# Inside a decoder layer: the order of an attention step, scores first and the turn of the probabilities last

## The chip, the cores and the metric

One core of a Trainium2 chip runs the whole kernel in one launch. The metric is the device time of one execution in microseconds (us); the kernel before was timed in three runs. Below, PE is the matrix engine and PEld its weight loads, DVE the vector engine, ACT the scalar engine, POOL the GpSimd engine and SP the queue that issues most DMAs.

## The reference

One decoder layer on 256 tokens with 16 learned meta tokens in front (T = 272 rows, width 2048, float32): a SwiGLU block, a merge of two mixers (differential attention and a short gated convolution), a second SwiGLU block, a last norm. The change lies in the attention. It has 8 heads, and each head has two score maps of 64-wide queries and keys and values 128 wide:

```
s = einsum('bqhcd,bkhcd->bchqk', q_blk, kp) * scale      # c = 0, 1
s = where(mask, s, NEG_INF)
p = softmax(s, axis=-1)
a = p[:, 0] - lam * p[:, 1]
out = einsum('bhqk,bkhv->bqhv', a, vp)
```

Before and after it stand plain matrix products: `h @ w_in` makes q, k, v and the three inputs of the convolution.

## The kernel before

**Dense products.** `linear` (L305) multiplies a 2048-deep activation with 512 columns of a weight matrix. Per 128-deep chunk it issues 12 matmuls (L367, L368, L369 for each of 4 column groups), because every float32 operand is split into a rounded high part and a low part. The weights come by DMA into `st`; for each block of two chunks ACT writes the high part `wh` (L351) and DVE the low part `wl` (L356), each in a ring of three buffers. A finished product stays in four of the eight PSUM banks until the next `linear` reaches its second chunk, where it is evicted (`flush`).

**Attention as side work.** The attention doesn't have a stage of its own. `side` is a list of small functions, and `linear` takes one from it after the chunks named in `side_at`, mostly every third chunk, so that a piece of attention lies after every 36 dense matmuls. The list holds 18 attention steps: the work is cut into 16 units, one for each head and each block of 128 queries (`qt` = 0 or 1), and step i works on three units at once (`att_step`, L999). Before the change it first multiplies the probabilities of unit i-2 with the values (`values`, L934), then transposes the probabilities of unit i-1 (`turn`, L919), and then makes the scores of unit i (`scores`, L889). The dense products in which these steps lie are the second k, the second v, and the first and second pair c and u of the convolution's inputs.

**A unit.** `scores` issues two matmuls on PE, one for each score map, with 64 rows of the array each (L896, out `sc_ps`); then DVE scales and masks them (L899, two instructions) and takes the row maxima (L903); ACT takes two exponentials with row sums (L906); DVE takes the reciprocals (L910), multiplies one with lambda (L911), scales the second map (L912) and combines the two maps by two instructions of line L914: one writes the 16 meta columns into `scM`, where four heads and both query blocks are gathered, and the other writes the 128 or 256 remaining columns back into `sc`. `turn` transposes these columns on PE (L923, out `aT`: one transpose for `qt` = 0, two for `qt` = 1) and ACT copies them to `aB` (L927). In the last unit of each group of four heads it also transposes `scM` (L925), which `meta_values` needs later. `values` multiplies `aB` with the values on PE (L938, out `po`: one or two matmuls), and DVE copies the result out (L939).

**What sets the order.** The program isn't run in the order in which it is written. A scheduler takes the instructions of each engine by the order in which they were recorded, but an instruction that by its own estimate isn't ready yet can be passed by later ones. On the chip each engine then works through its list in order and waits at semaphores. Pools with a fixed number of buffers (two for `sc`, eight PSUM banks for all products) add waits of their own.

Of the kernel before, what the change touches and what calls it, by code (L numbers as in the profile page):

```python
# [18 lines left out]
NMETA = 16  # L19
# [41 lines left out]
def decoder_layer(ctx: ExitStack, tc: tile.TileContext, t, out):  # L61
# [9 lines left out]
    def bank(name):  # L71
        return psum.tile([P, 512], F32, tag="acc", name=name)
# [579 lines left out]
    def mixed(plan, a, w, cols, name, end):  # L652

        ev = {}

        def done(k, ps):
            if k == "x":
                ev["u"] = wide([P, 2, GW], "u2x")
                nc.scalar.copy(out=ev["u"][:, 1, :], in_=ps)
            elif k == "3":  # L660
                ev["p3"] = ps
            elif k == "1":
                ev["e"], ev["g"] = wide([P, 2, GW], "cup"), wide([P, 2, GW], "cgate")
                nc.scalar.copy(out=ev["e"][:, 0, :], in_=ps)
            if k in "x31":
                return
            up, gt, u = ev["e"], ev["g"], ev["u"]
            if k == "2":
                nc.vector.tensor_add(gt[:, 0, :], ps, up[:, 0, :])
            elif k == "6":  # L670
                nc.vector.tensor_add(u[:, 0, :], ps, up[:, 0, :])
            elif k == "4":
                nc.vector.tensor_add(gt[:, 1, :], ps, u[:, 0, :])
            elif k == "5":
                nc.vector.tensor_sub(up[:, 0, :], ps, u[:, 0, :])
                nc.vector.tensor_add(up[:, 1, :], up[:, 0, :], u[:, 1, :])
                nc.vector.tensor_add(up[:, 0, :], ev["p3"], up[:, 0, :])
            elif k == "7":
                nc.vector.tensor_add(gt[:, 1, :], ps, gt[:, 1, :])
                nc.vector.tensor_sub(up[:, 1, :], up[:, 1, :], ps)  # L680

                pending.append(lambda: end(gt, up))

        linear_mix(plan, a, w, cols, name, done)
# [131 lines left out]
    def k_evict(g):  # L816
        def f(ps):
            kT[g] = apool.tile([P, GC, T], F32, tag="act", name=f"kT{g}")
            for j in range(GC):
                nc.vector.tensor_mul(kT[g][:, j, :], ps[j][:, :T], norm2.rstd)  # L820

        return f
# [23 lines left out]
    def v_evict(g):  # L846
        def f(ps):
            vt = wide([P, GC, T], "vt")
            for j in range(GC):
                nc.vector.tensor_mul(vt[:, j, :], ps[j][:, :T], norm2.rstd)  # L850
            steps = []

            def meta():
                vz = wide([P, GC, 2, GC, NMETA], "vz")
                nc.vector.memset(vz, 0.0)
                pa = bank("pa")
                for j in range(GC):
                    for i in range(2):
                        nc.vector.tensor_copy(vz[:, j, i, j, :], vt[:, j, :NMETA])
                    nc.tensor.transpose(  # L860
                        pa[:, j * P : (j + 1) * P], vz[:, j, :, :, :].rearrange("p i c m -> p (i c m)"), ident
                    )
                nc.vector.tensor_copy(vB[:, g, :, :].rearrange("p c v -> p (c v)"), pa)

            def real(i):
                pv = bank("pv")
                for j in range(GC):
                    nc.tensor.transpose(pv[:, j * P : (j + 1) * P], vt[:, j, NMETA + i * P : NMETA + (i + 1) * P], ident)
                nc.scalar.copy(out=vN[g][:, i, :, :].rearrange("p c v -> p (c v)"), in_=pv)

            def all_():
                meta()
                real(0)
                real(1)

            side.insert(0, all_)

        return f

    scM = [const.tile([P, 2, GC, NMETA], F32, name=f"scM{g}") for g in range(2)]  # L880
    aM = [None, None]

    class Unit:
# [5 lines left out]
        def scores(self):  # L889
            qt, g, j = self.qt, self.g, self.j  # L890
            nk = NMETA + (qt + 1) * P
            sc = tmp.tile([P, 2, T + NMETA], F32, tag="sc", name="sc")
            for c in range(2):
                rows = slice(c * HD, (c + 1) * HD)
                ps = bank("sc_ps")
                nc.tensor.matmul(  # L896
                    ps[:, :nk], qT[g][rows, j, qt * P : (qt + 1) * P], kT[g][rows, j, :nk], start=True, stop=True
                )
                nc.vector.scalar_tensor_tensor(  # L899
                    out=sc[:, c, :nk], in0=ps[:, :nk], scalar=rq[:, qt : qt + 1], in1=mask[:, T - nk :], op0=ALU.mult, op1=ALU.add  # L900
                )
            mx = tmp.tile([P, 2], F32, tag="mx", name="mx")
            nc.vector.tensor_reduce(out=mx, in_=sc[:, :, :nk], axis=AX.X, op=ALU.max, negate=True)  # L903
            sm = tmp.tile([P, 2], F32, tag="sm", name="sm")
            for c in range(2):
                nc.scalar.activation(  # L906
                    sc[:, c, :nk], sc[:, c, :nk], AF.Exp, bias=mx[:, c : c + 1], accum_out=sm[:, c : c + 1]
                )
            rs = tmp.tile([P, 2], F32, tag="rs", name="rs")
            nc.vector.reciprocal(rs, sm)  # L910
            nc.vector.tensor_mul(rs[:, 1:2], rs[:, 1:2], lam)  # L911
            nc.vector.tensor_scalar_mul(sc[:, 1, :nk], sc[:, 1, :nk], rs[:, 1:2])  # L912
            for out_, ks in ((scM[g][:, qt, j, :], slice(0, NMETA)), (sc[:, 0, NMETA:nk], slice(NMETA, nk))):
                nc.vector.scalar_tensor_tensor(  # L914
                    out=out_, in0=sc[:, 0, ks], scalar=rs[:, 0:1], in1=sc[:, 1, ks], op0=ALU.mult, op1=ALU.subtract
                )
            self.sc = sc
# [23 lines left out]
    def meta_values(g):  # L941
        om = [bank(f"om{qt}") for qt in range(2)]
        for qt in range(2):
            rows = slice(qt * GC * NMETA, (qt + 1) * GC * NMETA)
            nc.tensor.matmul(
                om[qt], aM[g][rows, :], vB[rows, g, :, :].rearrange("p c v -> p (c v)"), start=True, stop=True
            )
        for qt in range(2):
            o = oN[g][:, qt, :, :].rearrange("p c v -> p (c v)")
            nc.vector.tensor_add(o, om[qt], o)  # L950
        head_squares(g, 0)

    def head_squares(g, qt):
        for j in range(GC):
            junk = tmp.tile([P, P], F32, tag="junk", bufs=1, name="junk")
            h = g * GC + j
            nc.scalar.activation(junk, oN[g][:, qt, j, :], AF.Square, accum_out=osq[:, qt, h : h + 1])
# [30 lines left out]
    for g in range(2):  # L988
        dense = dict(side_at=(2, 5, 8, 11, 14) if g else (4, 6, 8, 10, 12))
        linear(h2, allk, w_in, 0, W2 + g * GW, 0, T, "k", k_evict(g), **dense)  # L990
        if g == 0:
            mixed(Q, hm, w_in, (0, GW), "q", q_end)
            mixed(B_PLAN, hm, w_in, (3 * W2, 3 * W2 + GW), "b", b_end)
            dense = dict(later_at=(3, 5, 7, 9))
        linear(h2, allk, w_in, 0, 2 * W2 + g * GW, 0, T, "v", v_evict(g), **dense)
        if g == 0:
            units = [Unit(h, qt) for h in range(NH) for qt in range(2)]

            def att_step(i):  # L999
                def f():  # L1000
                    if 0 <= i - 2 < len(units):
                        units[i - 2].values()
                    if 0 <= i - 1 < len(units):
                        units[i - 1].turn()
                    if i < len(units):
                        units[i].scores()

                return f

            half = len(units) // 2  # L1010
            side.extend(att_step(i) for i in range(half + 2))
            side.append(lambda: meta_values(0))
            side.append(lambda f=att_step(half + 2): [head_squares(0, 1), f()])
            side.extend(att_step(i) for i in range(half + 3, len(units) + 2))
            side.append(lambda: meta_values(1))
            side.append(lambda: [head_squares(1, 1), att_norm()])
            side.extend(att_out(h) for h in range(0, NH, 2))
# [313 lines left out]
```

## Time and profile before

| | |
|---|---|
| median of three runs | 2152.15 us (2152.11 to 2152.21) |
| the profiled execution, its own time | 2152.49 us |
| its span, first to last instruction | 2150.7 us |
| granted PE clock | 0.999 |
| busy: PE, DVE, ACT, POOL | 2139.3, 1612.9, 1104.4, 79.3 us |
| DMA over the span | 439.70 MB, mean 204 GB/s |
| the stretch of the attention steps, 938 to 1075 us: busy PE, DVE, ACT | 135.15, 104.14, 70.34 of 137.00 us |

The profile's rows give a start in us from the span's beginning, a duration, the engine, the line, the operation with its output and inputs, and in brackets the idle time of the engine before it with what ended it. PE's rows start when a matmul starts; its ends are modelled and overlap the next start. A matmul of full float32 operands shows as two rows (x2 for one, x4 for two), a transpose as one, and a dense matmul as one.

### The profile page before, as it was taken

Reading aid. Unit: us, or ns where it says so; the run is one execution under the profiler, and the core shown is the slowest. Engines: PE = TensorE matmul, PEld = TensorE weight load, DVE = VectorE, ACT = ScalarE, POOL = GpSimd, SP = SyncE. Lnnn points to the kernel's source line nnn. Section 1 sums busy time; section 2 is a strip of 40 time slices with the busy share of each in tenths; the row PEclk is TensorE's granted clock in tenths of the full one; section 3 lists DMA queues with packets and bytes.
Section 4 is the critical chain, followed back from the end, with each engine's and each line's share of the span. In section 5 each row is a group of like instructions: output and inputs, shape, how many; then the busy total and the mean of one; then the engine's idle time right before and its main releaser. Section 6 shows DMA issues by size and latency. Waiting matters only on the chain.

```text
span 2150.7 us, 33079 instructions
## 1 busy us (share of the span) xinstructions
PE 2139.3 (99%) x13202; PEld 1929.4 (90%) x13202; DVE 1612.9 (75%) x2139; ACT 1104.4 (51%) x1391; POOL 79.3 (4%) x89
## 2 busy tenths in 40 slices
PE   9999999999999999999999999999999999999998
PEld 9999999999999998898998888888888888888887
DVE  8555554445555668867788888889999899988998
ACT  6344343344443455544545555557665566555665
POOL 0000000000000000000000000001100111002100
PEclk9999999999999999999999999999999999999999
DMA  7555555555555555544455555668886999779963
GB/s 257 176 177 178 177 182 178 179 180 180 181 178 177 177 177 193 179 159 137 157 180 191 196 197 195 215 199 255 271 256 201 287 284 277 233 221 306 291 206 137
DMA packets 200544, 439.70 MB, mean 204 GB/s; under 512 B 10493, under 2 KB 11206, under 8 KB 200390
## 3 DMA queue, kind: packets, MB, share of 16 engines
q1 hardware_dynamic: 184022, 398.13, 54.9%
q0 software_dynamic: 15904, 38.80, 8.2%
q8 instruction: 103, 1.69, 0.3%
q10 hardware_dynamic: 464, 0.66, 0.1%
q14 instruction: 51, 0.42, 0.1%
HBM read 431.26 MB, written 2.10 MB: 201 GB/s over the span
## 4 chain that ended last, share of the span: by engine, by line
PE 96%; DVE 2%; ACT 1%; issue 0%; DMA 0%; SPq 0%; ACTq 0%
PE pg L569 6%; PE pg L571 6%; PE pg L570 6%; PE pd L369 4%; PE pd L367 4%; PE pu L369 4%; PE pu L367 4%; PE pu L368 4%; PE pd L368 4%; PE pg L369 4%; PE pg L367 4%; PE pg L368 4%; PE pd L571 4%; PE pd L569 4%; PE pd L570 4%; PE g L571 2%
## 5 line engine op out<-in xcount | busy, mean ns | idle before, releaser
L356 DVE TENSOR_TENSOR wl<-st,wh 128x1024 fp32r<-128x1024 f32 (+1 forms) x329 | 401.0, 1220 | 374.6 <-ACT wh L351 374.5
L351 ACT CAST wh<-st 128x1024 fp32r<-128x1024 f32 (+1 forms) x328 | 342.9, 1046 | 486.0 <-PE pu L368 151.0
L476 DVE TENSOR_TENSOR wl<-st,wh 128x1024 fp32r<-128x1024 f32 (+1 forms) x424 | 470.6, 1117 | 55.6 <-ACT wh L475 52.5
L475 ACT CAST wh<-st 128x1024 fp32r<-128x1024 f32 (+1 forms) x424 | 400.5, 970 | 209.3 <-PE pdx L570 59.3
L475 ACT CAST wh<-t 128x1024 fp32r<-128x1024 f32 x160 | 166.6, 1052 | 241.9 <-DVE t L609 154.1
L476 DVE TENSOR_TENSOR wl<-t,wh 128x1024 fp32r<-128x1024 f32 x160 | 193.8, 1221 | 56.7 <-ACT wh L475 52.7
L369 PE MATMUL pd<-mh,wl 128*128 128x272 f32 x704 | 203.3, 289 | 0.0
L367 PE MATMUL pd<-mh,wh 128*128 128x272 f32 x704 | 202.5, 288 | 0.0
L367 PE MATMUL pg<-h,wh 128*128 128x272 f32 x704 | 202.0, 288 | 0.4 <-ACT wh L351 0.3
L367 PE MATMUL pu<-h,wh 128*128 128x272 f32 x704 | 202.1, 287 | 0.0
L369 PE MATMUL pu<-h,wl 128*128 128x272 f32 x704 | 201.9, 287 | 0.0
L368 PE MATMUL pu<-h,wh 128*128 128x272 f32 x704 | 201.9, 287 | 0.0
L368 PE MATMUL pg<-h,wh 128*128 128x272 f32 x704 | 201.4, 287 | 0.0
L368 PE MATMUL pd<-ml,wh 128*128 128x272 f32 x704 | 200.9, 285 | 0.0
L369 PE MATMUL pg<-h,wl 128*128 128x272 f32 x704 | 199.9, 288 | 0.1
L570 PE MATMUL pg<-wh,h 128*128 128x512 f32 x399 | 156.1, 391 | 0.0
L569 PE MATMUL pg<-wh,h 128*128 128x512 f32 x399 | 155.9, 391 | 0.0
L571 PE MATMUL pg<-wl,h 128*128 128x512 f32 x399 | 155.8, 391 | 0.0
L367 PEld LDWEIGHTS pg<-h,wh 128*128 128x128 f32 x704 | 132.8, 189 | 1.2 <-ACT wh L351 0.9
L368 PEld LDWEIGHTS pd<-ml,wh 128*128 128x128 f32 x704 | 133.6, 190 | 0.0
L368 PEld LDWEIGHTS pg<-h,wh 128*128 128x128 f32 x704 | 132.7, 188 | 0.2 <-DVE h L232 0.2
L367 PEld LDWEIGHTS pu<-h,wh 128*128 128x128 f32 x704 | 132.7, 188 | 0.0
(391 smaller groups left out, 4841.6 us busy)
## 6 DMA issues: line engine op xcount, KB each, us to landing
st<-in_ffn_w_gu_dram SPq DMA_DIRECT2D x183, 512.0 KB, 6.0
st<-in_ffn_w_down_dram SPq DMA_DIRECT2D x88, 1024.0 KB, 5.1
st<-in_ffn_w_gu_dram SPq DMA_DIRECT2D x84, 1024.0 KB, 4.9
st<-in_w_in_dram SPq DMA_DIRECT2D x48, 1024.0 KB, 5.0
st<-in_w_gate_dram SPq DMA_DIRECT2D x64, 512.0 KB, 4.2
t<-in_ffn_w_gu_dram POOLq DMA_DIRECT2D x64, 512.0 KB, 7.4
st<-in_w_branch_dram SPq DMA_DIRECT2D x32, 512.0 KB, 4.8
st<-in_w_out_dram SPq DMA_DIRECT2D x16, 1024.0 KB, 5.2
```

What stands on the lines that cost most here:

```text
L351: nc.scalar.copy(out=wh[:, :m, :], in_=sw)
L356: nc.vector.tensor_sub(wl[:, :m, :], sw, wh[:, :m, :].bitcast(F32))
L367: nc.tensor.matmul(a, wh[:, i, f], act.part(c, 0, t0, t1), start=first, stop=False)
L368: nc.tensor.matmul(a, wh[:, i, f], act.part(c, 1, t0, t1), start=False, stop=False)
L369: nc.tensor.matmul(a, wl[:, i, f], act.part(c, 0, t0, t1), start=False, stop=last)
L475: part_last[:] = [nc.scalar.copy(out=wh, in_=src).ins]
L476: part_last.append(nc.vector.tensor_sub(wl, src, wh.bitcast(F32)).ins)
L569: nc.tensor.matmul(ps[k], hi, wh, start=first, stop=False)
L570: nc.tensor.matmul(ps[k], lo, wh, start=False, stop=False)
L571: nc.tensor.matmul(ps[k], hi, wl, start=False, stop=left[k] == 0)
```

## The change

In `att_step` the scores of unit i are now recorded first, then the values of unit i-2, and the turn of unit i-1 last. In `scores` the two combinations of L914 change places: the 128 or 256 columns that `turn` reads are written first and the 16 meta columns behind them. Nothing is added or taken away.

```
-            for out_, ks in ((scM[g][:, qt, j, :], slice(0, NMETA)), (sc[:, 0, NMETA:nk], slice(NMETA, nk))):
+            for out_, ks in ((sc[:, 0, NMETA:nk], slice(NMETA, nk)), (scM[g][:, qt, j, :], slice(0, NMETA))):
                 nc.vector.scalar_tensor_tensor(
                     out=out_, in0=sc[:, 0, ks], scalar=rs[:, 0:1], in1=sc[:, 1, ks], op0=ALU.mult, op1=ALU.subtract
                 )
...
             def att_step(i):
                 def f():
+                    if i < len(units):
+                        units[i].scores()
                     if 0 <= i - 2 < len(units):
                         units[i - 2].values()
                     if 0 <= i - 1 < len(units):
                         units[i - 1].turn()
-                    if i < len(units):
-                        units[i].scores()
```

The scheduler carries this through PE's, DVE's and ACT's lists; those of POOL and SP stay as they were. The first place is PE's list at step 6, inside the second v product (`v_...` are its four accumulators, `h_128` the activation chunk). A "+" marks the rows of the changed kernel, a "-" those of before.

```order
 L368 MATMUL v_10133<-h_128,wh 128x272
 L369 MATMUL v_10133<-h_128,wl 128x272
+L896 MATMUL sc_ps<-kT_8874,qT_9204 128x144 x2
 L938 MATMUL po<-vN_8499,aB 128x128
+L923 MATMUL aT<-ident,sc 128x128 x2
 L367 MATMUL v_10130<-h_128,wh 128x272
-L923 MATMUL aT<-ident,sc 128x128 x2
-L896 MATMUL sc_ps<-kT_8874,qT_9204 128x144 x2
 L368 MATMUL v_10130<-h_128,wh 128x272
```

The scores now stand at the head of the step, and one dense matmul that stood ahead of the transposes stands behind them. In eight of the sixteen steps that have a turn the list before had dense matmuls between the step's place and the transposes: 9 in step 1 (ahead of the whole group), then 4, 1, 1, 12, 8, 5 and 3 in steps 2, 6, 8, 12, 13, 14 and 16. In the changed list there are none in any step.

The second place is DVE's list from the end of unit 4's combination to the end of unit 5's, which the transposes of step 6 read. This is the list before:

```order
L356 TENSOR_TENSOR wl<-st,wh 128x1024
L939 COPY oN_8501<-po 128x128
L356 TENSOR_TENSOR wl<-st,wh 128x1024
L899 SCALAR_TENSOR_TENSOR sc<-sc_ps,rq,mask 128x272 x2
L903 TENSOR_REDUCE mx<-sc 128x2
L910 RECIPROCAL rs<-sm 128x2
L911 TENSOR_TENSOR rs<-rs,lam 128x1
L912 TENSOR_SCALAR sc<-sc,rs 128x272
L914 SCALAR_TENSOR_TENSOR scM_8504<-sc,rs 128x16
L914 SCALAR_TENSOR_TENSOR sc<-sc,rs 128x256
```

And this is the same place in the changed kernel:

```order
L356 TENSOR_TENSOR wl<-st,wh 128x1024
L899 SCALAR_TENSOR_TENSOR sc<-sc_ps,rq,mask 128x272 x2
L939 COPY oN_8501<-po 128x128
L903 TENSOR_REDUCE mx<-sc 128x2
L356 TENSOR_TENSOR wl<-st,wh 128x1024
L910 RECIPROCAL rs<-sm 128x2
L911 TENSOR_TENSOR rs<-rs,lam 128x1
L912 TENSOR_SCALAR sc<-sc,rs 128x272
L914 SCALAR_TENSOR_TENSOR sc<-sc,rs 128x256
L914 SCALAR_TENSOR_TENSOR scM_8504<-sc,rs 128x16
```

The copy of `po` and the second split `wl`, which stood ahead of the masking (L899), now stand behind it, the split behind the maxima (L903).

The third place is DVE's list at the end of unit 11's softmax, where the first c product is evicted (L1029, L1030). Before:

```order
L910 RECIPROCAL rs<-sm 128x2
L356 TENSOR_TENSOR wl<-st,wh 128x1024
L911 TENSOR_TENSOR rs<-rs,lam 128x1
L1030 TENSOR_TENSOR cg<-cg,rstd 128x258
L912 TENSOR_SCALAR sc<-sc,rs 128x272
L356 TENSOR_TENSOR wl<-st,wh 128x1024
L914 SCALAR_TENSOR_TENSOR scM_8505<-sc,rs 128x16
L914 SCALAR_TENSOR_TENSOR sc<-sc,rs 128x256
```

And in the changed kernel:

```order
L910 RECIPROCAL rs<-sm 128x2
L1029 TENSOR_TENSOR cg<-c_10512,rstd 128x258
L911 TENSOR_TENSOR rs<-rs,lam 128x1
L1029 TENSOR_TENSOR cg<-c_10513,rstd 128x258
L912 TENSOR_SCALAR sc<-sc,rs 128x272
L1030 TENSOR_TENSOR cg<-cg,rstd 128x258
L914 SCALAR_TENSOR_TENSOR sc<-sc,rs 128x256
L914 SCALAR_TENSOR_TENSOR scM_8505<-sc,rs 128x16
L1030 TENSOR_TENSOR cg<-cg,rstd 128x258
L356 TENSOR_TENSOR wl<-st,wh 128x1024 x2
```

Two splits that stood ahead of the combination now stand behind it.

More of the change, by code (lines that the diff above doesn't have):

```diff
@@ L912, in scores @@
             nc.vector.tensor_scalar_mul(sc[:, 1, :nk], sc[:, 1, :nk], rs[:, 1:2])
-            for out_, ks in ((scM[g][:, qt, j, :], slice(0, NMETA)), (sc[:, 0, NMETA:nk], slice(NMETA, nk))):
+            for out_, ks in ((sc[:, 0, NMETA:nk], slice(NMETA, nk)), (scM[g][:, qt, j, :], slice(0, NMETA))):
                 nc.vector.scalar_tensor_tensor(
@@ L1000, in f @@
                 def f():
+                    if i < len(units):
+                        units[i].scores()
                     if 0 <= i - 2 < len(units):
@@ L1004, in f @@
                         units[i - 1].turn()
-                    if i < len(units):
-                        units[i].scores()
                 return f
```

## Prediction

> **What bounds the kernel now.** I began with the profile's page: the span, the busy time of each engine, and the chain that ended last.
>
> ```profile
> span 2150.7 us, 33079 instructions
> PE 2139.3 (99%) x13202; PEld 1929.4 (90%) x13202; DVE 1612.9 (75%) x2139; ACT 1104.4 (51%) x1391; POOL 79.3 (4%) x89
> PE 96%; DVE 2%; ACT 1%; issue 0%; DMA 0%; SPq 0%; ACTq 0%
> ```
>
> PE is the bound: 96% of the chain is its own. The change adds and removes no matmul, so it can gain only what PE loses between matmuls, and only in the stretch with the attention steps. The second view is the list of what PE waits for.
>
> ```profile
> PE aT L923 <- DVE sc L914: 1.5, 6, 0.5
> ```
>
> In the attention steps it names one wait, that of the transposes of `turn` for the combined probabilities: 1.5 us in 6 steps. The wait is real, but this number is too small, as the third view shows, the timeline of PE's starts. First two steps without a wait, one of each kind: step 3, which makes the scores of a late query block and turns an early one, and step 4, the other way round.
>
> ```profile
> 957.32 0.28 PE L368 MATMUL k<-h,wh 128*128 128x272 f32 x1
> 957.44 0.29 PE L369 MATMUL k<-h,wl 128*128 128x272 f32 x1
> 957.57 0.61 PE L938 MATMUL po<-vN,aB 128*128 128x128 f32 x4
> 958.01 0.27 PE L923 MATMUL aT<-ident,sc 128*128 128x128 f32 x1
> 958.22 0.73 PE L896 MATMUL sc_ps<-kT,qT 64*128 64x272 f32 x4
> 958.88 0.39 PE L367 MATMUL k<-h,wh 128*128 128x272 f32 x1
> 959.10 0.29 PE L368 MATMUL k<-h,wh 128*128 128x272 f32 x1
> ```
>
> ```profile
> 964.91 0.38 PE L938 MATMUL po<-vN,aB 128*128 128x128 f32 x2
> 965.13 0.38 PE L923 MATMUL aT<-ident,sc 128*128 128x128 f32 x2
> 965.44 0.52 PE L896 MATMUL sc_ps<-kT,qT 64*128 64x144 f32 x4
> 965.88 0.39 PE L367 MATMUL v<-h,wh 128*128 128x272 f32 x1
> 966.11 0.28 PE L368 MATMUL v<-h,wh 128*128 128x272 f32 x1
> ```
>
> Read the starts, not the durations, which overlap. A dense matmul starts 0.12 us after the one before it (957.32, 957.44). Step 3 takes 959.10 - 957.57 = 1.53 us with one dense matmul inside, so 1.41 without it: values 0.44, transpose about 0.12, scores 0.85 (0.66, and 0.10 at each border, where 0.21 and 0.22 stand instead of 0.11 and 0.12). Step 4 takes 1.20 - 0.12 = 1.08: values 0.22, transposes 0.21, scores 0.65. Now step 6, which has the work of step 4:
>
> ```profile
> 976.29 0.38 PE L938 MATMUL po<-vN,aB 128*128 128x128 f32 x2
> 976.43 0.37 PE L367 MATMUL v<-h,wh 128*128 128x272 f32 x1
> 977.26 0.41 PE L923 MATMUL aT<-ident,sc 128*128 128x128 f32 x2 [0.46 <-DVE sc L914]
> 977.60 0.52 PE L896 MATMUL sc_ps<-kT,qT 64*128 64x144 f32 x4
> 978.04 0.40 PE L368 MATMUL v<-h,wh 128*128 128x272 f32 x1
> 978.28 0.29 PE L369 MATMUL v<-h,wl 128*128 128x272 f32 x1
> ```
>
> It takes 1.99 us with two dense matmuls, 1.75 without them: 0.67 more than step 4. The row's bracket says 0.46, because it counts from the modelled end of the matmul before. By the same subtraction ten of the sixteen steps with a turn are longer than a step without a wait: steps 2, 6, 7, 8, 11, 12, 13, 14, 15 and 16, by 0.41, 0.67, 0.33, 0.30, 0.47, 0.33, 0.31, 0.36, 0.38 and 0.18 us, 3.7 us in all. The other six have nothing to give. Here are the gaps ahead of the transposes in the first and the last of the ten.
>
> ```profile
> 952.24 0.29 PE L367 MATMUL k<-h,wh 128*128 128x272 f32 x1
> 952.73 0.41 PE L923 MATMUL aT<-ident,sc 128*128 128x128 f32 x2 [0.20 <-DVE sc L914]
> ```
>
> ```profile
> 1049.80 0.28 PE L369 MATMUL u<-h,wl 128*128 128x258 f32 x1
> 1050.06 0.41 PE L923 MATMUL aT<-ident,sc 128*128 128x128 f32 x2
> ```
>
> The last one carries no bracket, though 0.26 lie between the starts and not 0.12. The Trainium skill says the same of the record in "Perfetto Trace Analysis", section "Tensor Engine Instruction (MATMUL, LD_WEIGHTS)": the end time of a TensorE instruction is computed by the profiler, not observed. By idle time as recorded the change could give at most 1.5 us, by the starts 3.7; I take the starts.
>
> **Why the transposes wait.** DVE's timeline from step 5 to step 6 shows the softmax of unit 5.
>
> ```profile
> 971.08 0.29 DVE L939 COPY oN<-po 128x128 f32<-128x128 f32 x1 [0.57 <-PE po L938]
> 971.64 1.23 DVE L356 TENSOR_TENSOR wl<-st,wh 128x1024 fp32r<-128x1024 f32 x1 [0.27 <-ACT wh L351]
> 972.78 0.90 DVE L899 SCALAR_TENSOR_TENSOR sc<-sc_ps,rq,mask 128x272 f32<-128x272 f32 x2
> 973.72 0.72 DVE L903 TENSOR_REDUCE mx<-sc 128x2 f32<-128x544 f32 x1
> 975.69 0.17 DVE L910 RECIPROCAL rs<-sm 128x2 f32<-128x2 f32 x1 [1.25 <-ACT sc L906]
> ...
> 976.48 0.23 DVE L914 SCALAR_TENSOR_TENSOR scM<-sc,rs 128x16 f32<-128x16 f32 x1
> 976.63 0.48 DVE L914 SCALAR_TENSOR_TENSOR sc<-sc,rs 128x256 f32<-128x256 f32 x1
> ```
>
> The combination ends at 977.11 and the transposes start 0.15 us later. In step 2 they would be due at 952.36, in step 6 at 976.63: the chain of scores, maxima, exponentials and combination is some tenths longer than the 36 dense matmuls that lie between two steps, and a split of 1.14 us stands inside it.
>
> **The change, part by part.**
>
> *Meta columns behind the others.* The combination that PE waits for starts 976.63 - 976.48 = 0.15 us sooner in each step. What is late next is the meta columns, later by 0.4; only L925 reads them, in steps 8 and 16, behind two transposes of 0.21. Cost 0 to 0.1 us once or twice; I take nothing.
>
> *Scores first.* In the new step the scores start 0.43 us (965.44 - 964.91 - 0.10) or 0.55 us (958.22 - 957.57 - 0.10) sooner after the step's place, so the softmax can start sooner; and the next transposes stand behind the scores and the values, which cover them with 0.65 or 0.85 us of PE work. Worked through for unit 5, by the new list of DVE, in which the copy and the second split stand behind the masking; PE's row of step 5 and the free case from scores to masking are these. Step 5 begins at 970.43, and PE starts its scores 0.10 later.
>
> ```profile
> 970.43 0.61 PE L938 MATMUL po<-vN,aB 128*128 128x128 f32 x4
> ```
>
> ```profile
> 958.98 0.91 DVE L899 SCALAR_TENSOR_TENSOR sc<-sc_ps,rq,mask 128x272 f32<-128x272 f32 x2 [0.25 <-PE sc_ps L896]
> ```
>
> There the masking starts 0.76 after the scores (958.22), so here at 971.3; the maxima 0.94 later plus 0.25 for the copy, at 972.5; the reciprocal 1.97 after them (975.69 - 973.72; the split of 1.14 fits beside ACT's exponentials), at 974.45; the combination 0.94 - 0.15 later, at 975.25, ready at 975.75 and seen by PE 0.15 later, at 975.9. The transposes come due at 976.29 (the step's place) + 0.65 + 0.22 = 977.15. So they have 1.2 us in hand, where they were late by 0.67. Units with an early block run the same instructions over 144 columns instead of 272, which can only be shorter.
>
> *The dense matmuls that covered the transposes.* Here the new order gives something back: the 4, 1, 1, 12, 8, 5 and 3 dense matmuls that stood ahead of the transposes of steps 2, 6, 8, 12, 13, 14 and 16 now stand behind them. The worst place is step 12 with 12 of them, 1.43 us. There unit 11's chain on DVE also loses two splits (1.14 each) from its middle, as the third place of the order shows, so the combination comes about 2 x 1.14 + 0.15 = 2.4 us sooner and the cover isn't missed. If no chain came sooner at all, each stall would change by the cover lost less the scores that now stand ahead: 0.41 + 0.49 - 0.65 = 0.25 in step 2, then 0.14, 0, 0, 0, 0.33 + 1.43 - 0.65 = 1.11 in step 12, 0.41, 0.31, 0 and 0.54 in step 16, which has no scores: 2.7 us stay of 3.7. That bounds the gain from below at 1.0 us, as far as the waits go.
>
> *New borders on PE.* The scores use 64 rows of the array. Before, they stood between transposes and dense matmuls; now dense matmuls come ahead of them and values behind. The border ahead is in the trace, in step 0:
>
> ```profile
> 941.02 0.29 PE L369 MATMUL k<-h,wl 128*128 128x272 f32 x1
> 941.24 0.52 PE L896 MATMUL sc_ps<-kT,qT 64*128 64x144 f32 x4
> ```
>
> It is 0.22, again 0.10 above a dense start: as before. The border from scores to values isn't in the trace. From below it costs nothing, which would save 0.10 in 15 steps, 1.5 us. From above it adds the weight loads of the two float32 halves of `po`, if neither can be drawn ahead of the scores' end; this is their row in the view by tile (shortest, median and longest in ns):
>
> ```profile
> L938 PEld LDWEIGHTS po<-vN,aB x48: 187/189/193, 951.5 to 1061.7; 128*128 128x128 f32 x48
> ```
>
> That is up to 2 x 0.19 = 0.38 in 14 steps, 5.3 us. I take the usual 0.10, and so no change, since that is what scores into dense cost. The Trainium skill bears on this in "TensorEngine Tiling (Array Packing)", section "Key Properties": changing the tiling mode drains the engine. By that rule each step pays two drains in either order, so the sum stays.
>
> *DVE's and ACT's lists.* The copy of `po` (L939) moves behind the masking, by up to 0.9 us; its reader comes many steps later, and its bank is wanted a step later: nothing. The splits `wl` move back by at most 2.4 us; behind them PE would wait, but each is made with a ring of three blocks of 24 matmuls, and the list of PE's waits names no split: nothing. Were a split late by all of its 2.4 us beyond its ring, that would be lost once. The queues of SP and POOL are untouched.
>
> **The sum.** 3.7 us of stalls, less 0.3 for places with little in hand (step 2, whose whole group also comes 9 dense matmuls sooner after step 0, keeps perhaps 0.1 to 0.3 of its 0.41): 3.4 us. The profiled execution took 2152.49 us (1.8 outside its span), 0.34 above the median of the runs, so 2149.1 for it and 2148.7 us for the median. I call a change under 0.2% (4.3 us) the same, as a measurement of this kernel can tell about that much; the forecast of -0.16% lies within.
>
> **The rivals.**
>
> *The chains come no sooner* (12 in 100). If DVE's splits, which wait for ACT (the bracket at 971.64), held up the masking as they do now, only the cover would count and 1.0 us would be won: 2151.2 us. Against it: in the new list the second split stands behind L899 and L903.
>
> *The scores' border with the values costs more* (5 in 100). A price above 3.4 / 14 = 0.24 us per step turns the gain into a loss. At 0.38, 5.3 - 3.4 = 1.9 us slower, 2154.0. It would show as values starting late after the scores in every step.
>
> *The border is cheaper* (8 in 100). If scores into values cost no border, 1.5 us come on top, and the whole 3.7 us go: 2152.15 - 5.2 = 2146.9, faster by 0.24%.
>
> *The change does nothing* (3 in 100): 2152.1, if PE's gaps at the transposes had another cause than the combination. Against it stands the bracket at 977.26, which names it.
>
> **How the numbers follow.** The forecast with its 3.4 us has 72 in 100. The range reaches from 4.75 us of gain, the forecast with most of the border's 1.5 us, to the rival with 1.0 and a little less: 2147.4 to 2151.4. It leaves out the two borders' full prices and the change that does nothing, 16 in 100, and a few for the tails. Faster by over 0.2% needs 4.3 us, more than all stalls: only the cheap border gives it, 0.08. Slower by over 0.2% needs 7.7 us lost against the forecast, more than the dear border at its full price: 0.02, with a place I have not seen. The rest, 0.90, is the same.
>
> **What would show it.** Right: in the changed profile PE's wait for L914 is gone or under 0.3 us; the even steps take 1.08 and the odd ones 1.41 us of PE beside dense matmuls, with starts 0.44 or 0.66 us apart from scores to values and 0.1 between values and transposes; L899 starts under 0.9 us after the scores. Wrong: gaps of more than 0.2 us ahead of L923 in more than three steps, a gap behind L896 above the usual 0.1, a PE wait for `wl`, or a gain that PE's starts don't account for.

## The result, and the profile after

| | before | changed |
|---|---|---|
| median (all runs), us | 2152.32 (2152.06 to 2152.56) | 2149.17 (2148.85 to 2149.47) |
| ratio | | 0.9985, 95% interval 0.9979 to 0.9992 |
| profiled execution, its span, us | 2152.49, 2150.7 | 2149.04, 2147.3 |

The changed kernel is 3.15 us faster where 3.4 were forecast (2149.17 against 2148.7 us). The kernel before came out 0.17 us higher here than in the three runs from which the forecast starts. The page shows the same kernel as before, with a PE that is a little fuller; these are its span, its first busy row and the head of its chain.

```profile
span 2147.3 us, 33079 instructions
...
PE 2137.4 (100%) x13202; PEld 1929.1 (90%) x13202; DVE 1611.9 (75%) x2139; ACT 1105.5 (51%) x1391; POOL 79.4 (4%) x89
...
PE 98%; DVE 1%; DMA 0%; ACT 0%; issue 0%; SPq 0%; ACTq 0%
```

The list of PE's waits has lost its row for the combination (L914). These three rows are all that it has now (us in total, times, longest), and none of them lies in the attention steps.

```profile
PE warm L86 <- DVE ones L80: 1.1, 1, 1.1
PE pt L733 <- DMA xin<-in_x_dram: 0.5, 2, 0.3
PE pg L367 <- ACT h L231: 0.2, 1, 0.2
```

PE's timeline of step 6, the step that lost 0.67 us before, and the dense matmuls ahead of it:

```profile
971.33 0.37 PE L367 MATMUL v<-h,wh 128*128 128x272 f32 x1
...
975.85 0.29 PE L369 MATMUL v<-h,wl 128*128 128x272 f32 x1
976.06 0.52 PE L896 MATMUL sc_ps<-kT,qT 64*128 64x144 f32 x4
976.51 0.49 PE L938 MATMUL po<-vN,aB 128*128 128x128 f32 x2
976.83 0.38 PE L923 MATMUL aT<-ident,sc 128*128 128x128 f32 x2
976.97 0.37 PE L367 MATMUL v<-h,wh 128*128 128x272 f32 x1
977.18 0.29 PE L368 MATMUL v<-h,wh 128*128 128x272 f32 x1
...
981.38 0.28 PE L369 MATMUL v<-h,wl 128*128 128x272 f32 x1
```

From 975.85 to 977.18 are 1.33 us with two dense starts in them (two times 0.12): 1.09 us of side work, against 1.75 before. The same subtraction gives 1.07 to 1.09 in the even steps from 2 to 14, 1.41 in the odd ones from 3 to 15, 1.19 in step 8 (which also transposes `scM`) and 0.55 in step 16 (which has no scores); that is their work without a wait.

DVE's timeline for unit 5, whose probabilities step 6 transposes:

```profile
970.86 0.91 DVE L899 SCALAR_TENSOR_TENSOR sc<-sc_ps,rq,mask 128x272 f32<-128x272 f32 x2 [0.96 <-PE sc_ps L896]
971.68 0.28 DVE L939 COPY oN<-po 128x128 f32<-128x128 f32 x1
971.88 0.71 DVE L903 TENSOR_REDUCE mx<-sc 128x2 f32<-128x544 f32 x1
972.50 1.22 DVE L356 TENSOR_TENSOR wl<-st,wh 128x1024 fp32r<-128x1024 f32 x1
973.78 0.17 DVE L910 RECIPROCAL rs<-sm 128x2 f32<-128x2 f32 x1
...
974.57 0.48 DVE L914 SCALAR_TENSOR_TENSOR sc<-sc,rs 128x256 f32<-128x256 f32 x1
974.97 0.23 DVE L914 SCALAR_TENSOR_TENSOR scM<-sc,rs 128x16 f32<-128x16 f32 x1
```

The masking now waits for PE's scores and no longer behind the copy and the split. The columns for the transposes are ready at 974.57 + 0.48 = 975.05, and the transposes start at 976.83, 1.78 us later. In the kernel before, the ten late transposes started 0.14 to 0.15 us after the end of that combination; that is the time from DVE's end to PE's start, and what a distance has beyond it is time in hand. In the changed kernel the sixteen distances are 0.93, 0.20, 2.79, 1.94, 2.68, 1.78, 2.70, 1.72, 9.22, 7.05, 2.75, 2.26, 0.47, 1.48, 2.43 and 0.80 us: none waits. The nearest is step 2 with about 0.05 us in hand:

```profile
951.63 0.48 DVE L914 SCALAR_TENSOR_TENSOR sc<-sc,rs 128x256 f32<-128x256 f32 x1
951.99 0.49 PE L938 MATMUL po<-vN,aB 128*128 128x128 f32 x2
952.03 0.23 DVE L914 SCALAR_TENSOR_TENSOR scM<-sc,rs 128x16 f32<-128x16 f32 x1
...
952.31 0.38 PE L923 MATMUL aT<-ident,sc 128*128 128x128 f32 x2
```

To set kernels side by side without what happens elsewhere in the program, one stretch is measured in each, from the start of step 0's scores to the second dense matmul behind the second `meta_values`: 941.24 to 1067.63 in the kernel before, 126.39 us, and 941.09 to 1064.26 in the changed kernel, 123.17 us. The difference of 3.22 us is, within 0.1, the whole gain of the medians (3.15).

### The profile page after: what moved, and what is told of

The parts are those of the page before. It is cut to its first block, busy times and chain, and to the rows that moved or that the text cites. A ratio compares the mean times of both kernels' runs of the same rounds, so it can differ in the third digit from the quotient of the medians.

```text
span 2147.3 us, 33079 instructions
## 1 busy us (share of the span) xinstructions
PE 2137.4 (100%) x13202; PEld 1929.1 (90%) x13202; DVE 1611.9 (75%) x2139; ACT 1105.5 (51%) x1391; POOL 79.4 (4%) x89
## 4 chain that ended last, share of the span: by engine, by line
PE 98%; DVE 1%; DMA 0%; ACT 0%; issue 0%; SPq 0%; ACTq 0%
PE pg L569 6%; PE pg L571 6%; PE pg L570 6%; PE pd L369 4%; PE pd L367 4%; PE pu L367 4%; PE pu L368 4%; PE pu L369 4%; PE pd L368 4%; PE pg L367 4%; PE pg L368 4%; PE pg L369 4%; PE pd L571 4%; PE pd L570 4%; PE pd L569 4%; PE g L571 2%
```

## Theory, rivals and experiments

The theory: the gain is the ten waits of the transposes (3.7 us), and it is the order of the step that ends them, since the scores start sooner and then cover the transposes. Rival A: a good part of it comes from the exchange of the two combinations in L914. Rival B: it doesn't come from the wait at all, but from PE's new grouping, as the list no longer puts dense matmuls inside a step and the borders lie elsewhere. Further rivals stand in the expectations of the runs that test them.

The waits by step, each from PE's starts as above (us; a dot is under 0.03):

| step | 2 | 6 | 7 | 8 | 11 | 12 | 13 | 14 | 15 | 16 | sum | stretch |
|---|---|---|---|---|---|---|---|---|---|---|---|---|
| before | .41 | .67 | .33 | .30 | .47 | .33 | .31 | .36 | .38 | .18 | 3.74 | 126.39 |
| changed | . | . | . | . | . | . | . | . | . | . | . | 123.17 |
| 1 order alone | .13 | . | . | . | . | . | . | . | . | . | .13 | 123.17 |
| 2 L914 alone | .26 | .64 | .20 | .43 | .35 | .46 | .29 | .27 | .24 | .30 | 3.44 | 126.04 |
| 3 wait taken away | . | . | . | .08 | . | . | . | . | . | .25 | .33 | 123.14 |
| 4 values last | .24 | . | . | . | . | . | . | . | . | .56 | .80 | 122.82 |
| 5 mixed | . | . | . | . | . | . | . | . | . | .35 | .35 | 122.56 |
| 6 turn first | .25 | .61 | .39 | .48 | .78 | .18 | .31 | .46 | . | 1.49 | 4.95 | 127.90 |

**1. The order alone.** The diff of `att_step` as in the change; L914 stays as before.

> The new order of the step alone; the two combinations of L914 stay as before (meta columns first). Theory (the gain is the ten waits of the transposes for the combined probabilities, and the scores ahead of them remove these): the combination is ready 0.15 us later than in the changed kernel, where it has 0.05 us in hand in step 2, 0.32 in step 13 and more elsewhere, so at most 0.1 us comes back: 2149.3 us (2149.0 to 2149.6), all steps but one as clean as in the changed kernel. Rival A (half of the gain or more is the exchange in L914): 2150.7 us or more.

2149.11 us (2148.77 to 2149.19), ratio 0.9985 (0.9976 to 0.9993), as the theory has it. The order alone gives all of the gain, and rival A falls. Step 2 waits 0.13 us, which is what the exchange saves there in the full change; its combination ends at 951.91 + 0.48 = 952.39, and the transposes start 0.14 us later:

```profile
951.91 0.48 DVE L914 SCALAR_TENSOR_TENSOR sc<-sc,rs 128x256 f32<-128x256 f32 x1
952.53 0.41 PE L923 MATMUL aT<-ident,sc 128*128 128x128 f32 x2
```

**2. The exchange in L914 alone.**

```
-for out_, ks in ((scM[...], slice(0, NMETA)), (sc[:, 0, NMETA:nk], slice(NMETA, nk))):
+for out_, ks in ((sc[:, 0, NMETA:nk], slice(NMETA, nk)), (scM[...], slice(0, NMETA))):
```

> The exchange of the two combinations of L914 alone; the step stays values, turn, scores. Theory: each of the ten waits would shrink by 0.15 us, 1.5 in all, but the scheduler also takes back some of the dense matmuls that stood ahead of the transposes (9 over the steps, 1.1 us): the waits fall from 3.7 to 3.3 us, so 2151.9 us (2150.7 to 2152.3). Rival A: 2150.7 us or less.

2152.08 us (2151.76 to 2152.74), ratio 0.9999 (0.999 to 1.0008): nearly nothing, as the theory has it. The list of PE's waits now names the meta columns:

```profile
PE aT L923 <- DVE scM L914: 1.1, 4, 0.4
```

That name misleads, as the timeline of DVE and PE at step 6 shows:

```profile
976.85 0.48 DVE L914 SCALAR_TENSOR_TENSOR sc<-sc,rs 128x256 f32<-128x256 f32 x1
977.25 0.23 DVE L914 SCALAR_TENSOR_TENSOR scM<-sc,rs 128x16 f32<-128x16 f32 x1
...
977.48 0.41 PE L923 MATMUL aT<-ident,sc 128*128 128x128 f32 x2 [0.44 <-DVE scM L914]
```

The transposes start 0.15 us after the end of `sc` (977.33), as in the kernel before, and at the very moment at which `scM` ends, which they don't read (L923 reads `sc` alone): they are released by `sc`, and so 0.15 us sooner after the reciprocal than in the kernel before. The steps whose list is unchanged gain about that: 0.13, 0.12 and 0.14 in steps 7, 11 and 15. In the seven others the scheduler's list puts fewer dense matmuls between the step's place and the transposes (3 where 4 stood in step 2, none where 1 stood in steps 6 and 8, 11 for 12, 6 for 8, 3 for 5 and 2 for 3 in steps 12, 13, 14 and 16), and each one fewer is 0.12 us of cover lost; those steps range from 0.15 gained to 0.13 lost. So what would be 1.5 us in ten waits became 0.3 us; how the 1.2 divide between the lost cover and other moves of the list was not taken apart.

**3. The wait taken away, in the order of the kernel before.** The transposes read queries that were loaded long before; the output of the attention is then not the reference's.

```
-nc.tensor.transpose(pa[...], sc[:, 0, NMETA + i * P : NMETA + (i + 1) * P], ident)
+nc.tensor.transpose(pa[...], qT[self.g][:, self.j, i * P : (i + 1) * P], ident)
```

> The kernel before in its old order, with the wait taken away by other data: the transposes L923 read a block of the queries, long ready, instead of the combined probabilities, so the attention's output is not the reference's; every instruction stays. Theory: the ten waits go without any new order, 3.7 us: 2148.6 to 2149.2 us. Rival B (the new place of the scores on PE, its borders and the closed group, makes the gain, and the wait is only how it looks in the record): little over half of the gain at most, 2150.8 us or more.

2149.25 us (2148.78 to 2151.1), ratio 0.9987 (0.9978 to 0.9995), 0.05 us above the range. Its profiled execution began the stretch 1.8 us later, after a longer wait for ACT at the kernel's start, so the stretch is what counts: 123.14 us, against 123.17 of the changed kernel. PE's timeline of step 6:

```profile
977.69 0.38 PE L938 MATMUL po<-vN,aB 128*128 128x128 f32 x2
977.91 0.38 PE L923 MATMUL aT<-ident,qT 128*128 128x128 f32 x2
978.22 0.52 PE L896 MATMUL sc_ps<-kT,qT 64*128 64x144 f32 x4
978.67 0.39 PE L367 MATMUL v<-h,wh 128*128 128x272 f32 x1
```

Same order as before, transposes 0.22 us behind the values, and no wait. Only the transposes of `scM` (L925), which still read the softmax's result, wait by 0.08 in step 8 and 0.25 in step 16. Taking away 3.4 us of waits wins 3.25 us of the stretch, and a new order of the step isn't needed for it: rival B's borders fall. One half of it stays open here, since this kernel's list, too, has no dense matmuls inside a step; experiment 8 answers that.

**4. Values last.** Scores, turn, values: the transposes lose the cover of the values.

```
 if i < len(units):
     units[i].scores()
+if 0 <= i - 1 < len(units):
+    units[i - 1].turn()
 if 0 <= i - 2 < len(units):
     units[i - 2].values()
-if 0 <= i - 1 < len(units):
-    units[i - 1].turn()
```

> Scores, then the turn, then the values: the transposes lose the cover of the values, 0.22 or 0.44 us. Theory: the changed kernel has more than that in hand in all steps but 2 and 13, where 0.17 and 0.12 us of wait would come back: 2149.5 us (2149.2 to 2149.7). Side question: in the changed kernel the 272-column dense matmuls start 0.1266 instead of 0.1235 us apart after the groups of steps 3, 5 and 7, which end with a single transpose, 0.4 us in all. If the end of the group makes that, values at the end bring it back: 2149.1 us; if not, it stays.

2148.68 us (2148.6 to 2149.34), ratio 0.9983 (0.9974 to 0.9992): below the changed kernel and below both numbers expected, by 0.4 us in the case that came true (with values at the end, the dense matmuls after the odd steps are fast again). PE's list has the waits back, and its timeline shows the larger one, in step 16, which has no scores to cover the transposes:

```profile
PE aT L923 <- DVE scM L914: 0.6, 2, 0.4
```

```profile
1045.32 0.28 PE L369 MATMUL u<-h,wl 128*128 128x258 f32 x1
1045.97 0.41 PE L923 MATMUL aT<-ident,sc 128*128 128x128 f32 x2 [0.38 <-DVE scM L914]
```

By starts it is 0.24 in step 2 and 0.56 in step 16, 0.8 us in all (0.17 in step 2 and 0.12 in step 13 were expected). Three things outweigh them. Each step from 2 to 15 has 0.04 us less work (1.05 and 1.37), 0.6 in all, which no theory had. The dense matmuls after the odd steps run faster. And a wait of 0.14 us for a split in the second c product, which the changed kernel has (shown below under "DVE's lists"), is gone. Step 5 and the last dense matmul of its run:

```profile
970.27 0.73 PE L896 MATMUL sc_ps<-kT,qT 64*128 64x272 f32 x4
970.93 0.33 PE L923 MATMUL aT<-ident,sc 128*128 128x128 f32 x1
971.10 0.61 PE L938 MATMUL po<-vN,aB 128*128 128x128 f32 x4
971.46 0.37 PE L367 MATMUL v<-h,wh 128*128 128x272 f32 x1
...
975.87 0.29 PE L369 MATMUL v<-h,wl 128*128 128x272 f32 x1
```

The shorter step is the border behind the scores: 0.17 us lie between the start of the transpose and that of the values (970.93, 971.10), 0.05 above the 0.11 that is usual, where with values or dense matmuls behind the scores it is 0.10.

The run of 36 dense matmuls takes 975.87 - 971.46 = 4.41 us. In the changed kernel the run at the same place took 975.85 - 971.33 = 4.52 (quoted with step 6 above), though the one after step 6 took 981.38 - 976.97 = 4.41. So this is where the changed kernel gave something back: over the stretch the 294 steps from one dense matmul of 272 columns to the next, those next to side work left out, take 36.66 us, and in experiments 3 and 4 the same number takes 36.29 in each. (That experiment 3 and the changed kernel have nearly the same stretch comes from such small things: the one still waits 0.33 us at its transposes, the other has 0.37 us of slower dense matmuls and the 0.14 at the split.)

**5. The mixture.** Values last, but ahead of the turn in step 2 and from step 16 on, where cover is short.

```
 if i < len(units):
     units[i].scores()
+late = i != 2 and i < len(units)
+if late and 0 <= i - 1:
+    units[i - 1].turn()
 if 0 <= i - 2 < len(units):
     units[i - 2].values()
-if 0 <= i - 1 < len(units):
+if not late and 0 <= i - 1 < len(units):
     units[i - 1].turn()
```

> Scores, turn, values as in the run before with values last, but the values ahead of the turn again in the steps where its trace shows a wait: step 2 (0.24 us) and the two last steps, which have no scores (0.56 us). Theory: the values' cover of 0.22 us removes the 0.24 and, with the place in the list that it gives back, most of the 0.56; nothing else moves: 0.5 to 0.8 us under the values-last order, 2148.0 us (2147.8 to 2148.4), 4.3 us under the kernel before. Rival E (what differs between these orders is only the jitter of the start): 2148.7 to 2149.2 us.

2148.51 us (2148.31 to 2148.84), ratio 0.9982 (0.9973 to 0.9991), 0.1 us above the range given, and 0.17 below experiment 4 where 0.5 to 0.8 were expected. It has the lowest median, 3.85 us below the kernel before and 0.66 below the changed kernel; its runs overlap with those of experiment 4. The number lies between the theory's range and that of rival E, and the profiled stretches (122.56 against 122.82 us) are one execution of each. Two parts were missed. Step 16 keeps 0.35 of its 0.56, because the values cover only 0.22 us there. And the wait for the split that experiment 4 didn't have is back, with 0.21 us: two starts of dense matmuls lie 0.22 us apart at 1053.22 to 1053.67, where 0.12 is usual. Step 2 is clean (1.09).

**6. Turn first.** Turn, values, scores, with the exchange in L914: the transposes get no cover at all.

```
-if 0 <= i - 2 < len(units):
-    units[i - 2].values()
 if 0 <= i - 1 < len(units):
     units[i - 1].turn()
+if 0 <= i - 2 < len(units):
+    units[i - 2].values()
 if i < len(units):
     units[i].scores()
```

> Turn, then values, then scores, the exchange in L914 kept. Theory: the transposes lose the cover of the values (0.22 or 0.44 us) and get neither the scores' cover nor an earlier chain; by the dense matmuls that the list puts between one step's scores and the next step's transposes, the ten waits sum to some 4.2 us instead of 3.7: 2152.8 us (2152.0 to 2153.5). Rival F (any order in which the scheduler is given the turn anew gives a clean list): 2149.2 us.

2154.02 us (2153.7 to 2154.44), ratio 1.0007 (0.9998 to 1.0016): slower by 1.7 us, in the direction of the theory and 0.5 us above its range; the rival in the expectation falls. PE's list of waits:

```profile
PE aT L923 <- DVE scM L914: 3.1, 6, 1.3
```

By starts it is 5.0 us in the steps and another 0.2 at the eviction of v (L860, L868). What was mis-sized is above all step 16, 1.49 us: there neither scores nor values nor dense matmuls stand ahead of the transposes, while evictions of the u product (L1035, L1037) stand between the reciprocal and the combination on DVE.

**7 and 8. A longer chain.** In the changed kernel, ACT copies the second score map onto itself, twice or five times, between the exponentials and the reciprocal. One copy takes 0.30 to 0.42 us, median 0.36. (Lines behind it are 2 higher: the transposes are L925, the values L940, the combination L916.)

```
+for _ in range(2):      # 5 in experiment 8
+    nc.scalar.copy(out=sc[:, 1, :nk], in_=sc[:, 1, :nk])
 rs = ...
 nc.vector.reciprocal(rs, sm)
```

> The changed kernel with two copies in place on ACT in each softmax, behind the exponentials (the values stay the same); about 0.3 us each for 272 columns and 0.25 for 144, worked out from the exponentials' rows (0.53 and 0.43 apart with the sums). The scheduler's list on PE stays. Theory: only steps with less in hand wait, step 2 by some 0.55 us and step 13 by 0.2: 2149.9 us (2149.5 to 2150.5). Rival D (the waits are only just avoided everywhere): 0.5 us in each of 14 steps, 2156 us.

2149.67 us (2149.39 to 2149.93), ratio 0.9987 (0.9978 to 0.9996): 0.5 us above the changed kernel, within the range. The size is right by luck, since the place isn't: the wait stands in step 1 (0.32), where the list put 15 dense matmuls ahead of the transpose although the expectation let the list stay; step 2 waits 0.04, all other steps are clean, and the wait for the split in the c product is 0.28 instead of 0.14. So from step 3 on 0.7 us more of chain is paid from what is in hand, though not in a plain subtraction: in step 13, where a wait was expected, the distance grew from 0.47 to 0.73.

> The same with five copies, 1.25 to 1.5 us. Here the scheduler itself puts 2 to 13, mostly 10 to 13, dense matmuls ahead of the transposes again, as in the list before the change. Theory: these cover 1.2 to 1.5 us and the changed order has 0.3 to 2.5 in hand, so few waits come back and a split group costs nothing by itself: 2149.2 to 2151.0 us. Rival B (the closed group on PE is what gains): 2151.5 us or more even where no transposes wait.

2152.73 us (2152.41 to 2153.35), ratio 1.0001 (0.9992 to 1.001): missed, above what the theory gave; the number alone would fit rival B, and it is the steps that tell the two apart. Five copies are 1.8 us of chain (five times 0.36) where 1.25 to 1.5 were expected, and with them the waits are back. PE's list, and its timeline at steps 5 and 6:

```profile
PE aT L925 <- DVE scM L916: 1.2, 6, 0.2
...
PE aT L925 <- DVE sc L916: 0.4, 1, 0.4
```

```profile
973.22 0.29 PE L368 MATMUL v<-h,wh 128*128 128x272 f32 x1
973.70 0.30 PE L925 MATMUL aT<-ident,sc 128*128 128x128 f32 x1 [0.19 <-DVE scM L916]
973.75 0.38 PE L369 MATMUL v<-h,wl 128*128 128x272 f32 x1
...
977.02 0.52 PE L896 MATMUL sc_ps<-kT,qT 64*128 64x144 f32 x4
977.47 0.49 PE L940 MATMUL po<-vN,aB 128*128 128x128 f32 x2
977.71 0.37 PE L367 MATMUL v<-h,wh 128*128 128x272 f32 x1
...
979.04 0.29 PE L368 MATMUL v<-h,wh 128*128 128x272 f32 x1
979.16 0.38 PE L925 MATMUL aT<-ident,sc 128*128 128x128 f32 x2
979.30 0.37 PE L369 MATMUL v<-h,wl 128*128 128x272 f32 x1
```

The list now puts mostly 10 to 13 dense matmuls ahead of the transposes (24 in steps 1 and 2, 2 in step 3, 3 in step 11, none in steps 9 and 10). Where the chain is still too long, the split step waits: 0.48 between 973.22 and 973.70 where 0.12 would do, and 0.35, 0.26, 0.30, 0.39, 0.37, 0.43, 0.44, 0.41 and 0.62 us more than its work in steps 1, 3, 4, 5, 7, 11, 13, 15 and 16. Where it isn't, as in step 6 (0.12 from 979.04 to 979.16), the split step costs 1.09 us, the same as an undivided one; steps 8, 12 and 14 cost 1.20, 1.09 and 1.08. A group that is split costs nothing by itself, and so the second half of rival B falls as well. And the loss comes back with a longer chain, in the new order of the step: it is the wait that costs.

## Why the prediction was right

*What bounds the kernel.* PE's gaps at the transposes were all that the change could move, and by the starts they held 3.7 us. Experiment 3 takes the waits away in the old order of the step and gains 3.25 in the stretch, twice what the recorded idle time (1.5 us) allows. The rule of the Trainium skill in "Perfetto Trace Analysis", section "Tensor Engine Instruction (MATMUL, LD_WEIGHTS)", that a matmul's end is computed, agrees with that: the sum by starts is the one that the time follows.

*Meta columns behind.* The release came 0.15 us sooner as worked out, and the meta columns cost nothing in steps 8 and 16. The full change needs it in one place, step 2. Alone it gained 0.3 us instead of the 1.5 of ten waits (experiment 2).

*Scores first.* Of unit 5's walk, the masking was forecast 0.87 us after the step's place and came at 970.86 - 969.99 = 0.87 (the place is 0.10 ahead of the scores at 970.09). The combination was ready 5.06 us after it, 0.26 sooner than worked out, and the slower dense matmuls put step 6 off by 0.11, so that 1.6 us were in hand instead of 1.2. Where unit 11's chain was to come 2.4 us sooner against the step's place, it came 3.2 sooner (1.81 us behind that place in the kernel before, 1.39 ahead of it now), and the twelve dense matmuls of cover in step 12 were not missed (2.26 us from ready to start).

*The cover that was given back.* Nothing of the 2.7 us that would have stayed if no chain came sooner did stay, and the rival with 1.0 us of gain falls: L899 starts 0.77 us after the scores.

*The border between scores and values.* The 0.10 that was taken is what it costs. In step 6 the values start 0.45 after the scores, as dense matmuls did (0.44), and the transposes 0.32 behind the values, 0.10 more than the 0.22 of step 4 in the kernel before; as with dense matmuls, the price shows one instruction behind the scores. Neither the free border nor the 0.38 came. The drain that the Trainium skill states in "TensorEngine Tiling (Array Packing)", section "Key Properties", agrees as far as the changed kernel goes: two borders per step in either order, at 0.10 us each. That the price is a drain, no run here shows, and it isn't the same before every neighbour: experiment 4 pays 0.05 where a transpose follows the scores.

*DVE's lists.* The list of PE's waits names no split and no bank, and "nothing" was still not quite right. By the starts PE waits once for a split `wl`, in the second c product behind step 16, where no start of the kernel before is late. These are rows of the changed kernel:

```profile
1052.70 1.22 DVE L356 TENSOR_TENSOR wl<-st,wh 128x1024 fp32r<-128x1024 f32 x1
1053.81 0.28 PE L368 MATMUL c<-h,wh 128*128 128x258 f32 x1
1053.97 0.39 PE L369 MATMUL c<-h,wl 128*128 128x258 f32 x1
1054.19 0.28 PE L367 MATMUL c<-h,wh 128*128 128x258 f32 x1
```

The split ends at 1053.92 and the matmul that reads it starts 0.05 us later. The two starts come 0.38 us after 1053.81 instead of 0.24, so this costs 0.14 us. It is one of the signs that the prediction named as wrong, at a small price.

*The sum, and the step of it that was wrong.* "Less 0.3 for places with little in hand (step 2 ... keeps perhaps 0.1 to 0.3 of its 0.41)" failed: step 2 keeps nothing, by about 0.05 us. Its reason was misread, too: it is step 1's group, not step 2's, that comes 9 dense matmuls sooner after step 0 (36 of them instead of 45), so 36 instead of 27 lie between step 1's scores and step 2, and unit 1's chain has more time. What makes step 2 the nearest is that DVE still has two splits inside that chain (at 947.76 and 949.70, around the maxima) where unit 5's has one. All 3.74 us of waits went. In that term's place stood two costs that the prediction did not have: the slower dense matmuls after steps 3, 5 and 7, 36.66 - 36.29 = 0.37 us, and the 0.14 at the split. So -3.74 + 0.37 + 0.14 = -3.23 for the stretch, measured -3.22; the term's size was nearly right and its reason wrong, so that part of the number is luck. The gain of 0.15% is within the 0.2% that the text calls the same; the free border, which alone could have carried it beyond, did not come.

## What to carry to other kernels

When an engine that bounds the kernel waits for a chain through other engines, put work that is ready ahead of the instruction that waits, and above all the work that starts the next turn of that chain: it gains twice, as cover and as an earlier start (how the gain divides between the two was not taken apart here). Measure such waits from start to start against a step that doesn't wait, not by the idle time of the record. And where a scheduler writes the list, an earlier release can be handed back, as in experiment 2: compare the lists before trusting a saved tenth.

## What the runs showed of the hardware beside that

- From the end of DVE's combination to the start of the transposes lie 0.14 to 0.15 us in each of the ten waits of the kernel before, in experiment 1's step 2 and in all ten of experiment 2. In the changed kernel, where no step waits, the distances are larger, 0.20 to 9.22. In experiment 2 this told the true releaser where the trace named another. It isn't a least value: in experiment 8's step 16, which waited 0.62 us, the distance is 0.06 (1051.07 to 1051.12).
- The border ahead of the 64-row scores costs 0.09 to 0.10 us, whether dense matmuls (0.22 from start to start where 0.12 is usual), values or transposes (0.21 and 0.20 where 0.11 is usual) stand there. The border behind them costs 0.10 before dense matmuls and values and 0.05 before transposes (experiment 4).
- So a step with the transposes right behind the scores and the values last is 0.04 us shorter than one with the transposes last (1.05 and 1.37 against 1.08 and 1.41).
- Runs of dense matmuls of 272 columns go slower in some places: 36 in 4.52 us instead of 4.41 after steps 5 and 7, and 48 in 6.04 instead of 5.90 after step 3, all behind odd steps that end with four value matmuls and a single transpose. With the values last it is gone (4.41 after step 5 in experiment 4), and experiment 1, with the same order inside these steps, had it after steps 5 and 7 but not after step 3. No wait and no lower granted clock (1.00 in these runs, 0.999 over the span) goes with it; its cause stays open and wasn't tried.
